# The gated linear unit of two S5 layers: seven products of halves in place of two column passes

## The chip, the cores and the metric

The kernel runs on one core of a Trainium2 chip. TensorE (PE) multiplies, VectorE (DVE) and ScalarE (ACT) work element by element, GpSimd (POOL) does a little arithmetic and issues transfers, and SyncE (SP) only issues transfers. The metric is the time of one launch in device microseconds; a shown time is the median of several runs, and the profile is one separate execution.

## The reference

The kernel is a trunk of four layers for one sequence of 512 tokens and 1024 features, in float32. Layers 0 and 3 mix with S5, layer 1 with gated linear attention, layer 2 with differential attention; behind every mixer comes a feed-forward network (FFN). The change concerns the end of the S5 mixer:

```python
    y = y + d_skip.astype(f32) * h.astype(f32)
    z = jax.nn.gelu(y).astype(h.dtype)
    a, b = jnp.split(z @ w_glu, 2, axis=-1)
    return a * jax.nn.sigmoid(b)
...
    x = x + mix.astype(x.dtype)
    h = rmsnorm(x, norm_ffn[layer])
    x = x + swiglu_ffn(h, ffn_w_gate_up[layer], ffn_w_down[layer]).astype(x.dtype)
```

z is 512 x 1024 and w_glu is 1024 x 2048: columns 0 to 1023 give the values a, columns 1024 to 2047 the gates b.

## The kernel before

Every float32 matmul is done in parts. A weight tile is loaded by SP (`staged`, L357), ACT writes its rounded high part (`high`, L368), and DVE writes the rest as the low part (`low`, L376). `mm3` (L396 to L398) then multiplies high by high, high by low and low by high into one PSUM bank. The transposed z (`zT`) is kept in both parts. One weight tile of two blocks of 128 rows by 512 columns (512 KB, an element count of 128x1024) serves 2 x 4 x 3 = 24 matmuls of 128x512: two blocks of K, four blocks of 128 tokens (t), three part products. A pass over 512 columns is four such tiles, 96 matmuls.

The GLU has four passes. The first (gate columns 1024 to 1535) runs inside the S5 code before; `s5_glu` receives its four banks and takes their tanh. Then come, in `s5_glu`: value columns 0 to 511, gate columns 1536 to 2047, and value columns 512 to 1023. Sigmoid is written with tanh. Behind a value pass DVE multiplies (L1884) and adds the result to the residual x (L1886). For each t the updated x goes on into the FFN's left side (`Sides`): ACT squares it for the norm (L114), PE transposes it in four pieces (`put`, L123, into one of two `tp` banks), ACT scales the pieces from PSUM into `halves` (`keep`, L211), and once two t are there, their high and low parts are made (L206, L207). The FFN's own matmuls (L565) are already seven products of halves.

The program order of every engine in `s5_glu` is set by a scheduler from dependences up to the last pass's tail; from there it is written out (`hand_all` in `gemm_b`'s tail), the first two FFN weight tiles are staged and split ahead of that tail (`ahead(2)`), and the last four blocks of K are done t by t, so that x of t = 0 is ready while PE still multiplies for the other t. FFN weights that are sums of two tiles come as a plain load by SP and a second, accumulating transfer issued by POOL (L598, L601).

## Time and profile before

| | |
|---|---|
| median of 3 runs | 2273.99 us (2273.94 to 2277.14) |
| the profiled execution | 2275.25 us, of which its span 2273.2 us |
| granted TensorE clock | 0.991 |
| busy share of the span | PE 97%, DVE 69%, ACT 49%, POOL 12% |
| GLU of layer 0 in `s5_glu` | about 157 to 226 us of the span |
| GLU of layer 3 in `s5_glu` | about 1855 to 1924 us |

A row of the timeline gives the start, the duration, the engine, the source line, the operation, the tile written and the tiles read, and in brackets the engine's idle time before it and what ended that. A row of the groups gives busy time and the mean of one, then the idle time before. Tile names have no numbers there. PE matmuls are pipelined: a row's duration is longer than the step from one to the next. In a windows row stand the busy time and the number of instructions of PE, PE's weight loads, DVE, ACT and POOL, the granted clock, the busy share of the transfer engines and the rate.

### The profile page before, as it was taken

To read this page: it belongs to the slowest core of one execution; us is meant where nothing else is said; L and a number is where in the kernel's file an instruction comes from. 1 tells how busy PE (TensorE), PEld (TensorE's weight loads), DVE (VectorE), ACT (ScalarE), POOL (GpSimd) and SP (SyncE) were. 2 spreads that over 40 slices of the span, in tenths; PEclk is the share of its full clock that TensorE was granted. 3 is DMA by queue.
4 is the path that set the end of the run, shared out by engine and by line. 5 is a ranking of instruction groups with operands and counts; after the bars stand their busy time and mean duration, and the time that the engine had idled before them with its cause. 6 is when DMAs were issued, how large, how long until landed. Compare 5 with 4: busy or idle time off the path is not lost.

```text
span 2273.2 us, 37225 instructions
## 1 busy us (share of the span) xinstructions
PE 2201.9 (97%) x14847; PEld 1954.2 (86%) x14847; DVE 1561.0 (69%) x2420; ACT 1120.6 (49%) x1870; POOL 282.6 (12%) x392
## 2 busy tenths in 40 slices
PE   5999999999999999999999999999999899999997
PEld 3878979889777799998988887999998888989896
DVE  8963978776625479777745775977766954957574
ACT  6534645454453456555435675644444234635342
POOL 1000141521000011101002231111000001101000
PEclk8999999999999999999999999999999999999999
DMA  4257476663422557766237365976531646767521
GB/s 88 51 153 187 114 194 160 171 187 84 123 74 74 143 144 181 193 161 164 93 126 158 93 151 139 244 208 148 169 92 45 159 131 158 195 158 181 152 76 65
DMA packets 295463, 317.83 MB, mean 140 GB/s; under 512 B 72221, under 2 KB 235353, under 8 KB 294906
## 3 DMA queue, kind: packets, MB, share of 16 engines
q1 hardware_dynamic: 233050, 234.23, 34.1%
q0 software_dynamic: 62240, 81.22, 19.2%
q8 instruction: 117, 1.92, 0.4%
q14 instruction: 56, 0.46, 0.1%
HBM read 283.54 MB, written 16.65 MB: 132 GB/s over the span
## 4 chain that ended last, share of the span: by engine, by line
PE 82%; DVE 8%; ACT 4%; issue 3%; DMA 2%; SPq 1%; POOL 0%; ACTq 0%; DVEq 0%; POOLq 0%
PE a L565 18%; PE acc L396 14%; PE acc L398 13%; PE acc L397 13%; PE c L565 8%; PE d L565 4%; PE y L1481 2%; DVE whl L376 2%; ACT whl L368 1%; PE s L2309 1%; PE V L1445 1%; PE op L2343 1%; PE tp L123 1%; DVE halves L229 1%; ACT halves L211 1%
## 5 line engine op out<-in xcount | busy, mean ns | idle before, releaser
L376 DVE TENSOR_TENSOR whl<-wst,whl 128x1024 fp32r<-128x1024 f32 x272 | 331.4, 1223 | 258.1 <-ACT whl L368 257.1
L368 ACT CAST whl<-wst 128x1024 fp32r<-128x1024 f32 x272 | 283.9, 1050 | 306.8 <-PE acc L398 227.8
L565 PE MATMUL a<-side,whl 128*128 128x256 f32 x3168 | 382.7, 277 | 4.1 <-DVE whl L376 3.6
L565 PEld LDWEIGHTS a<-side,whl 128*128 128x128 f32 x3168 | 369.4, 188 | 6.9 <-DVE whl L376 5.5
L396 PE MATMUL acc<-whl,act 128*128 128x512 f32 x704 | 278.3, 396 | 1.7 <-DVE x L548 1.7
L397 PE MATMUL acc<-whl,act 128*128 128x512 f32 x704 | 274.7, 390 | 0.0
L398 PE MATMUL acc<-whl,act 128*128 128x512 f32 x704 | 274.6, 390 | 0.0
L565 PE MATMUL c<-side,whl 128*128 128x256 f32 x2112 | 254.3, 277 | 1.2 <-DVE whl L376 1.2
L565 PEld LDWEIGHTS c<-side,whl 128*128 128x128 f32 x2112 | 246.7, 188 | 2.0 <-DVE whl L376 2.0
L376 DVE TENSOR_TENSOR whl<-slot,whl 128x1024 fp32r<-128x1024 f32 x107 | 130.5, 1222 | 70.5 <-ACT whl L368 70.5
L396 PEld LDWEIGHTS acc<-whl,act 128*128 128x128 f32 x704 | 132.1, 188 | 32.1 <-issue 2.6
L398 PEld LDWEIGHTS acc<-whl,act 128*128 128x128 f32 x704 | 132.2, 188 | 27.9
L397 PEld LDWEIGHTS acc<-whl,act 128*128 128x128 f32 x704 | 132.2, 188 | 25.7
L368 ACT CAST whl<-slot 128x1024 fp32r<-128x1024 f32 x107 | 112.2, 1053 | 82.8 <-PE acc L398 35.1
L396 PE MATMUL acc<-whl,hT 128*128 128x512 f32 x352 | 142.3, 404 | 0.0
L398 PE MATMUL acc<-whl,hT 128*128 128x512 f32 x352 | 138.2, 393 | 0.0
L397 PE MATMUL acc<-whl,hT 128*128 128x512 f32 x352 | 138.0, 392 | 0.0
L565 PE MATMUL a<-sides,whl 128*128 128x256 f32 x1056 | 134.4, 283 | 0.0
L565 PEld LDWEIGHTS a<-sides,whl 128*128 128x128 f32 x1056 | 129.7, 191 | 1.1
L565 PE MATMUL d<-sides,whl 128*128 128x256 f32 x1056 | 126.6, 276 | 1.0 <-ACT whl L368 1.0
L565 PEld LDWEIGHTS d<-sides,whl 128*128 128x128 f32 x1056 | 122.9, 188 | 1.2 <-ACT whl L368 1.2
L704 ACT CAST act<-r 128x512 fp32r<-128x512 f32 (+1 forms) x110 | 66.4, 646 | 115.4 <-DVE r L683 108.0
(458 smaller groups left out, 3872.0 us busy)
## 6 DMA issues: line engine op xcount, KB each, us to landing
wst<-in_ffn_w_gate_up_dram SPq DMA_DIRECT2D x88, 512.0 KB, 5.0
wst<-in_ffn_w_down_dram SPq DMA_DIRECT2D x88, 512.0 KB, 4.2
slot<-in_ffn_w_gate_up_dram SPq DMA_DIRECT2D x71, 512.0 KB, 5.5
wst<-in_ffn_w_gate_up_dram POOLq DMA_DIRECT2D x44, 512.0 KB, 6.1
halves<-in_ffn_w_gate_up_dram SPq DMA_DIRECT2D x43, 512.0 KB, 5.4
wst<-in_s_w_glu_dram SPq DMA_DIRECT2D x32, 512.0 KB, 4.5
wst<-in_gla_w_in_dram SPq DMA_DIRECT2D x24, 512.0 KB, 3.7
wst<-in_diff_w_qkv_dram SPq DMA_DIRECT2D x24, 512.0 KB, 4.4
```

Of the source, the lines that this page charges most:

```text
L123: tr.nc.tensor.transpose(p[:, j], h[:, j * P : (j + 1) * P], tr.ident[:])
L211: self.tr.nc.scalar.mul(self.F[t // 2, d][:, j, (t % 2) * P : (t % 2 + 1) * P], p[:, j], self.gcol[:, 4 * d + j : 4 * d + j + 1])
L229: v.tensor_tensor(s, s, y, op=op)
L368: self.last["high"] = self.nc.scalar.copy(hl[:, 0], w[:])
L376: self.last["low"] = self.nc.vector.tensor_tensor(hl[:, 1], w[:], hl[:, 0].bitcast(F32), op=ALU.subtract)
L396: mm(out, lh, rh, start=first, stop=False)
L397: mm(out, lh, rl, start=False, stop=False)
L398: self.last["mm"] = mm(out, ll, rh, start=False, stop=last)
L565: mm(o, hl[:, x, k, c], side[y][:, k], start=first and not (j or k or n), stop=k == 3 and n == 2, skip_group_check=True,)
L704: self.last["act high"] = nc.scalar.copy(dst[:, 0, j], src[:, j])
L1445: mm(V[kk][z][:, bs(b)], inm[:, z, bs(b)], U[:, bs(b)], start=True, stop=True)
L1481: mm(yb[:, b], q[:, j, b], om[:, j // 2, bs(b)], start=False, stop=j == 3)
```

## The change

The first column pass in `s5_glu` (values 0 to 511, now L458 to L460) stays: 96 matmuls. The two passes over value columns 512 to 1023 and gate columns 1536 to 2047, 192 matmuls, become seven products of halves. Tokens are halved (t = 0, 1 and t = 2, 3), K is halved, and the two column blocks are the halves of the weight. Each product has 2 t x 4 blocks of K x 3 parts = 24 matmuls of 128x512 (L1986), 168 in all.

What feeds them is new. The class `WideSides` makes the left sides. POOL adds high and low of a quarter of zT back together (`joined`, L269), DVE forms the sums "1" to "4" (L287, L288, L293, L304), and ACT and DVE split each again (`parts`, L273, L274). The weights' sums are formed by transfers: SP loads a piece into `wsum` or `third` (L1974), POOL's accumulating transfer adds another (L1979), eight of these per layer. `wsum` holds in turn three sums (product "1", then "2", then "4"), each by accumulating on the last. `third` (product "3") is a new tile in the storage of `wide1`, the left side of product "1". Weight splits (L430 high, L438 low) are 18 per layer in place of 12. PSUM results are copied to SBUF by ACT (L1997) and combined by DVE (L2055, L2062, L2069); the gate (L1992, L1994) and the tanh (L1996) follow. `gated` now writes multiply and add for each t in turn. The two FFN heads (`ahead(2)`) are written before the combination r2. The order on all five engines is written out for the whole of `s5_glu`.

The order of the products on PE is: first pass, 11 ("11" is the weight piece and the left quarter), 1, 2, 12 with 21, 3, 4 with 22, 22 with the sum "4"; the transposes of x for the last three t stand inside or behind the last product.

Here is the diff, cut to its core:

```diff
+class WideSides:
...
+    def __init__(self, tr, pool, hT, spare):
+        self.tr, self.hT = tr, hT
+        self.m = pool.tile([P, 4, 256], F32, name="summand")
+        self.y = {n: pool.tile([P, 2, 4, 256], F32R, tag="wide" + n, name="wide" + n) for n in ("1", "4", "3", "2")}
+        self.s = spare[:].rearrange("p (k n) -> p k n", n=256)
...
+    def joined(self, out, name, ks=slice(0, 4)):
+        hi, lo = (self.quarter(name, z)[:, ks].bitcast(F32) for z in range(2))
+        self.tr.nc.gpsimd.tensor_tensor(out, hi, lo, op=ALU.add)
+    def parts(self, name, src, ks=slice(0, 4)):
+        hi, lo = (self.side(name, z)[:, ks] for z in range(2))
+        self.tr.nc.scalar.copy(hi, src)
+        self.tr.nc.vector.tensor_tensor(lo, src, hi.bitcast(F32), op=ALU.subtract)
+    def whole(self, then):
+        self.u = [(slice(k, k + 2), self.tr.np_.tile([P, 2, 256], F32, tag="hh", name="wideu")) for k in (0, 2)]
+        self.joined(self.m[:], "22")
+        self.joined(self.s, "21")
+        then()
+        for ks, u in self.u:
+            self.joined(u[:], "11", ks)
+    def first(self):
+        v = self.tr.nc.vector
+        for ks, u in self.u:
+            v.tensor_tensor(u[:], u[:], self.s[:, ks], op=ALU.subtract)
+        v.tensor_tensor(self.s, self.s, self.m[:], op=ALU.subtract)
+        self.parts("1", self.s)
+    def second(self):
+        for ks, u in self.u:
+            self.tr.nc.vector.scalar_tensor_tensor(
+                self.s[:, ks], u[:], -1.0, self.m[:, ks], op0=ALU.mult, op1=ALU.subtract
+            )
+        self.joined(self.m[:], "12")
+        self.parts("2", self.s)
+    def third(self):
+        for ks, u in self.u:
+            self.parts("3", u[:], ks)
+    def fourth(self):
+        self.tr.nc.vector.tensor_tensor(self.s, self.s, self.m[:], op=ALU.add)
+        self.parts("4", self.s)
...
         v = nc.vector
         wg = self.i["s5_w_glu"][L]
         nxt = Sides(self, 3 * L, self.i["ffn_w_gate_up"][3 * L])
+        mm = nc.tensor.matmul
+        cols = (512, D + 512)
+        self.hand_all()
         with self.tc.tile_pool(name=f"s5g_{L}", bufs=1) as p:
-            for d in range(2):
...
-                stat = lambda k, part, t: zT[:, part, k, t * P : (t + 1) * P]
-                if d == 0:
-                    for t in range(NT):
-                        evac_b(t, accs[t])
-                else:
-                    self.gemm_b(stat, wg, KT, D + d * 512, evac_b)
-                ahead = (lambda: (nxt.ahead(2), nxt.total("3"))) if d else None
-                with nullcontext() if d else self.tc.issue_after(self.last_turned.ins):
-                    self.gemm_b(stat, wg, KT, d * 512, evac_a, tail=4 if d else 0, ahead=ahead)
+            self.edge(p, 64)
...
+            sums = WideSides(self, p, zT, nxt.g)
+            wide = p.tile([P, 4, 512], F32, name="wsum")
+            half = lambda y, b: y[:, 2 * b : 2 * b + 2]
+            piece = lambda q, c, b: self.wb_src(wg, 4 * q + 2 * b, cols[c])
+            W, H = {}, {}
+            for b in range(2):
+                W[f"1{b}"] = W[f"2{b}"] = W[f"4{b}"] = half(wide, b)
+            def stage(*names):
+                for n in names:
+                    b = int(n[-1])
+                    src = self.wb_src(wg, 2 * b, 0) if n[0] == "w" else piece(int(n[0]) - 1, int(n[1]) - 1, b)
+                    W[n] = self.staged(src, 2, 512)
...
+            def both(y, name, one, two):
+                for b in range(2):
+                    nc.sync.dma_start(half(y, b), piece(*one, b))
+                return lambda: plus(y, two)
+            def plus(y, two):
+                for b in range(2):
+                    nc.gpsimd.dma_start(half(y, b), piece(*two, b), accum_op=ALU.add)
+            def product(side, name, bank, first, t, ks=range(4)):
+                st = sums.stat(side)
+                for k in ks:
+                    hl = H[name + str(k // 2)]
+                    for n, (x, y) in enumerate(((0, 0), (0, 1), (1, 0))):
+                        mm(
+                            bank[t][:], st(k, x, t), hl[:, y, k % 2], start=first and not (k or n),
+                            stop=k == 3 and n == 2, skip_group_check=True,
+                        )
+            def gated(t, d, th, value):
+                v.scalar_tensor_tensor(th, th, 1.0, value, op0=ALU.add, op1=ALU.mult)
+                xs = self.x[:, t, d * 512 : (d + 1) * 512]
+                v.scalar_tensor_tensor(xs, th, 0.5, xs, op0=ALU.mult, op1=ALU.add)
+            tanh = lambda y, src=None: nc.scalar.activation(y, y if src is None else src, AF.Tanh, scale=0.5)
+            copy = lambda y, bank: [nc.scalar.copy(y[z][:], bank[z][:]) for z in range(2)]
+            stage("w0", "w1", "w2")
+            summed = both(wide, "1", (0, 1), (0, 0))
+            sums.whole(summed)
+            split("w0", "w1")
+            for t in range(NT):
+                tanh(gate[t][:], accs[t][:])
+            stage("w3", "110", "111", "210")
+            split("w2", "w3", "110")
+            sums.first()
+            split("111")
+            sums.second()
+            split("10", "11")
+            plus(wide, (1, 1))
+            sums.third()
+            stage("211")
+            banks = [self.acc() for t in range(NT)]
+            for k in range(KT):
+                for t in range(NT):
+                    ts = slice(t * P, (t + 1) * P)
+                    hl = H[f"w{k // 2}"]
+                    self.mm3(
+                        banks[t][:], zT[:, 0, k, ts], zT[:, 1, k, ts], hl[:, 0, k % 2], hl[:, 1, k % 2],
+                        k == 0, k == KT - 1,
+                    )
+                    if k == KT - 1:
+                        gated(t, 0, gate[t][:], banks[t][:])
+                        nxt.take(t, 0)
+            r1, r5 = ([line("gate", 4) for z in range(2)] for y in range(2))
+            a, c = ([self.acc() for z in range(2)] for y in range(2))
+            d = [self.sbank("d") for z in range(2)]
+            product("11", "11", a, True, 0)
+            self.flush()
+            product("11", "11", a, True, 1)
+            split("210")
+            copy(r1, a)
+            split("20")
+            for t in range(2):
+                product("1", "1", c, True, t)
+            third = p.tile([P, 4, 512], F32, tag="wide1", name="third")
+            W.update({f"3{b}": half(third, b) for b in range(2)})
+            summed = both(third, "3", (0, 1), (1, 1))
+            stage("220", "221")
+            split("21")
+            sums.fourth()
+            copy(r5, c)
+            for t in range(2):
+                product("2", "2", a, False, t)
+            summed()
+            plus(wide, (1, 0))
+            split("211", "30")
+            copy(r2, a)
+            for t in range(2):
+                product("12", "21", d, True, t)
+            split("31", "220")
+            for z in range(2):
+                v.tensor_tensor(r1[z][:], r1[z][:], d[z][:], op=ALU.add)
+            split("221")
+            for t in range(2):
+                product("3", "3", a, False, t)
+            split("40")
+            nxt.total("3")
+            for z in range(2):
+                v.tensor_tensor(r5[z][:], r5[z][:], a[z][:], op=ALU.subtract)
+                tanh(r5[z][:])
+            split("41")
+            for t in range(2):
+                product("4", "22", c, False, t)
+            nxt.ahead(2)
+            for z in range(2):
+                v.tensor_tensor(r2[z][:], c[z][:], r2[z][:], op=ALU.subtract)
+                tanh(r2[z][:])
+                gated(z, 1, r2[z][:], r1[z][:])
+                if z == 0:
+                    nxt.take(0, 1)
+            product("22", "4", a, False, 0, range(2))
+            nxt.take(1, 1)
+            product("22", "4", a, False, 0, range(2, 4))
+            gated(2, 1, r5[0][:], a[0][:])
+            product("22", "4", a, False, 1, range(2))
+            nxt.take(2, 1)
+            product("22", "4", a, False, 1, range(2, 4))
+            gated(3, 1, r5[1][:], a[1][:])
+            nxt.take(3, 1)
         return nxt
```

**SP, the loads in the second half of the GLU of layer 0.** Rows with their waits: DVE, PE and Pool are engines, DMAHW and DMASW are transfers by SP and by POOL. `wst` is a staged weight, `slot0` an FFN weight. Before:

```order
L357 DMA wst_1824<-in_s5_w_glu_dram 128x2x512 [waits DMAHW6_49,DVE_49]
L357 DMA wst_1865<-in_s5_w_glu_dram 128x2x512 [waits DMAHW7_49,DVE_49]
L357 DMA wst_1894<-in_s5_w_glu_dram 128x2x512 [waits DMAHW0_49,DVE_49]
L357 DMA wst_1923<-in_s5_w_glu_dram 128x2x512 [waits DMAHW1_49,DVE_49]
L357 DMA wst_1928<-in_s5_w_glu_dram 128x2x512 [waits DMAHW2_49,DVE_49]
L357 DMA wst_1935<-in_ffn_w_gate_up_dram 128x4x256 [waits DMAHW3_49,DVE_49]
L357 DMA wst_1937<-in_ffn_w_gate_up_dram 128x4x256 [waits DMAHW4_49,DVE_49]
```

and now:

```order
L419 DMA wst_1598<-in_s5_w_glu_dram 128x2x512 [waits DMAHW7_49,DVE_49]
L419 DMA wst_1634<-in_s5_w_glu_dram 128x2x512 [waits DMAHW0_49,DVE_49]
L1974 DMA third_1856<-in_s5_w_glu_dram 128x2x512 [waits DVE_49,PE_49]
L1974 DMA third_1856<-in_s5_w_glu_dram 128x2x512 [waits DMAHW5_49]
L419 DMA wst_1859<-in_s5_w_glu_dram 128x2x512 [waits DMAHW6_49,DMAHW1_49,DVE_49]
L419 DMA wst_1861<-in_s5_w_glu_dram 128x2x512 [waits DMAHW2_49,DVE_49]
L419 DMA wst_2004<-in_ffn_w_gate_up_dram 128x4x256 [waits DMAHW3_49,DVE_49]
```

The loads of `third` wait for PE (the storage of `wide1`), and the weight loads for product "22" (1859, 1861) and the FFN's loads are queued behind them. The next place is ACT at the same point; 1902 and 1931 are the high parts of `third`, 1966 that of the last `wsum`, `r2` the copies of the accumulator that product "3" then adds to, gate_1774 and gate_1775 hold r5:

```order
L430 CAST whl_1899<-wst_1634 128x1024
L430 CAST whl_1902<-third_1856 128x1024
L1997 COPY r2_1558<-acc_1776 128x512
L1997 COPY r2_1559<-acc_1777 128x512
L430 CAST whl_1931<-third_1856 128x1024
L430 CAST whl_1934<-wst_1859 128x1024
L430 CAST whl_1939<-wst_1861 128x1024
L430 CAST whl_1966<-wsum_1565 128x1024
```

Before, ACT had only high parts of plain loads at this point. The copies of `r2` must come before product "3" adds on in the same banks, and they are queued behind the first high part of `third`.

**DVE, the last work before x of t = 0 of the second column half.** Before (1930 is the last weight of the GLU, 1939 and 1942 are the FFN's heads):

```order
L376 TENSOR_TENSOR whl_1930<-wst_1928,whl_1930 128x1024
L376 TENSOR_TENSOR whl_1939<-wst_1935,whl_1939 128x1024
L376 TENSOR_TENSOR whl_1942<-wst_1937,whl_1942 128x1024
L225 TENSOR_TENSOR s3_1945<-halves_1545 128x512
L225 TENSOR_TENSOR s3_1947<-halves_1545 128x512
L1884 SCALAR_TENSOR_TENSOR gate_1844<-gate_1844,acc_1861 128x512
L1886 SCALAR_TENSOR_TENSOR x_1541<-gate_1844,x_1541 128x512
```

and now (2008 and 2011 are the FFN's heads, 1966 and 1977 the low parts of the last `wsum`, `acc_1776` the bank of product "3", `acc_1778` that of product "4"):

```order
L438 TENSOR_TENSOR whl_1939<-wst_1861,whl_1939 128x1024
L438 TENSOR_TENSOR whl_1966<-wsum_1565,whl_1966 128x1024
L225 TENSOR_TENSOR s3_1969<-halves_1545 128x512
L225 TENSOR_TENSOR s3_1971<-halves_1545 128x512
L2062 TENSOR_TENSOR gate_1774<-gate_1774,acc_1776 128x512
L2062 TENSOR_TENSOR gate_1775<-gate_1775,acc_1777 128x512
L438 TENSOR_TENSOR whl_1977<-wsum_1565,whl_1977 128x1024
L438 TENSOR_TENSOR whl_2008<-wst_2004,whl_2008 128x1024
L438 TENSOR_TENSOR whl_2011<-wst_2006,whl_2011 128x1024
L2069 TENSOR_TENSOR r2_1558<-acc_1778,r2_1558 128x512
L1992 SCALAR_TENSOR_TENSOR r2_1558<-r2_1558,gate_1772 128x512
L1994 SCALAR_TENSOR_TENSOR x_1541<-r2_1558,x_1541 128x512
```

The FFN's heads stand between the last split and the first multiply in both, but two subtractions (L2062), a further split and the r2 subtraction (L2069) have come between.

**PE, behind the first column pass.** Before, `tp` for t = 0 and 1 follows the first matmul of the next pass:

```order
L398 MATMUL acc_1562<-whl_1652,zT_91 128x512
L396 MATMUL acc_1715<-whl_1721,zT_91 128x512
L123 MATMUL tp_1688<-ident_78,x_1541 128x128 x4
L123 MATMUL tp_1704<-ident_78,x_1541 128x128 x4
L397 MATMUL acc_1715<-whl_1721,zT_91 128x512
L398 MATMUL acc_1715<-whl_1721,zT_91 128x512
```

and now:

```order
L459 MATMUL acc_1638<-whl_1603,zT_91 128x512
L460 MATMUL acc_1638<-whl_1603,zT_91 128x512
L123 MATMUL tp_1745<-ident_78,x_1541 128x128 x4
L458 MATMUL acc_1639<-whl_1603,zT_91 128x512
L459 MATMUL acc_1639<-whl_1603,zT_91 128x512
L460 MATMUL acc_1639<-whl_1603,zT_91 128x512
L123 MATMUL tp_1761<-ident_78,x_1541 128x128 x4
L1986 MATMUL acc_1776<-whl_1606,zT_91 128x512 x6
L1986 MATMUL acc_1776<-whl_1614,zT_91 128x512 x6
L123 MATMUL tp_1794<-ident_78,x_1541 128x128 x4
L123 MATMUL tp_1803<-ident_78,x_1541 128x128 x4
```

The first transposes stand ahead of the last three matmuls of the pass, the second behind them, and the third and fourth 12 matmuls later, inside the first of the seven products.

30 lines of the change are left out of this document (21 added, 9 removed).

## The prediction

> **What bounds the kernel now.** I read the head of the page first, then the chain of waits, then windows around the GLU, then the timeline and groups there. The page:
>
> ```profile
> span 2273.2 us, 37225 instructions
> PE 2201.9 (97%) x14847; PEld 1954.2 (86%) x14847; DVE 1561.0 (69%) x2420; ACT 1120.6 (49%) x1870; POOL 282.6 (12%) x392
> PE 82%; DVE 8%; ACT 4%; issue 3%; DMA 2%; SPq 1%; POOL 0%; ACTq 0%; DVEq 0%; POOLq 0%
> ```
>
> PE bounds the whole. The windows show what that means at the change: the first pass of layer 0, its two last passes, the FFN behind it, and the last passes of layer 3.
>
> ```profile
> 157.00:179.00 22.00, 22.00 (x99) 18.22 (x98) 9.60 (x10) 7.37 (x9) 0.00 (x0) 1.00 0.60 186
> 179.00:227.00 48.00, 47.98 (x229) 39.71 (x228) 18.61 (x23) 22.17 (x53) 5.10 (x4) 1.00 0.77 200
> 227.00:262.00 35.00, 34.81 (x305) 34.62 (x304) 31.48 (x36) 22.19 (x33) 6.28 (x8) 1.00 0.41 95
> 1877.00:1925.00 48.00, 47.98 (x228) 39.69 (x227) 18.62 (x23) 21.85 (x52) 5.18 (x4) 1.00 0.71 180
> ```
>
> PE never stands still in either GLU and the clock is full: every matmul saved there is time, and every wait added is time. DVE works 28 of 70 us there. Behind it the FFN has 0.2 us of PE's idle time in 35, so it can give nothing back and hide nothing late.
>
> **What is removed.** The step of a 128x512 matmul comes from two rows of the timeline 12 matmuls apart:
>
> ```profile
> 215.23 0.39 PE L396 MATMUL acc<-whl,zT 128*128 128x512 f32 x1
> ...
> 217.95 0.39 PE L396 MATMUL acc<-whl,zT 128*128 128x512 f32 x1
> ```
>
> 2.72 / 12 = 0.227 us. Per layer 192 matmuls become 168: 24 x 0.227 = 5.4 us, 10.9 us for both. That is all the change can gain.
>
> **What is added, and whether it is hidden.** Prices of the element-wise work:
>
> ```profile
> L376 DVE TENSOR_TENSOR whl<-wst,whl 128x1024 fp32r<-128x1024 f32 x16 | 19.5, 1223 | 29.2 <-ACT whl L368 29.2
> L368 ACT CAST whl<-wst 128x1024 fp32r<-128x1024 f32 x16 | 16.7, 1051 | 26.5 <-PE acc L398 22.6 <-DMA wst<-in_s_w_glu_dram 3.9
> L114 ACT ACTIVATE sq<-x 128x512 f32<-128x512 f32 x8 | 5.0, 631 | 8.6 <-DVE x L1886 8.6
> L114 ACT ACTIVATION_READ_ACCUMULATOR sq<-x 128x1 f32 x8 | 1.5, 192 | 0.0
> L1881 ACT ACTIVATE gate<-acc 128x512 f32<-128x512 f32 x8 | 4.6, 600 | 2.6 <-PE acc L398 2.3
> ...
> 186.02 1.23 DVE L207 TENSOR_TENSOR sides<-halves,sides 128x1024 fp32r<-128x1024 f32 x1 [2.61 <-ACT sides L206]
> 187.16 1.22 DVE L376 TENSOR_TENSOR whl<-wst,whl 128x1024 fp32r<-128x1024 f32 x1
> 210.86 1.29 DVE L225 TENSOR_TENSOR s<-halves 128x512 f32<-128x512 f32 x2
> 217.52 0.69 DVE L1886 SCALAR_TENSOR_TENSOR x<-gate,x 128x512 f32<-128x512 f32 x1
> 219.32 0.60 PE L123 MATMUL tp<-ident,x 128*128 128x128 f32 x4
> 219.96 1.14 ACT L211 ACTIVATE halves<-tp,gffn 128x128 f32<-128x128 f32 x4 [0.99 <-PE tp L123]
> ```
>
> Back to back, a 1024-wide DVE operation steps by 1.14 (186.02 to 187.16), a 512-wide one by 0.62 to 0.65. Per layer DVE gets six weight splits, four side splits, the sums and six combinations, 18 to 20 us, ACT about 14. Both have that much room on average; where PE waits is a matter of place, and I went through the four places in program order.
>
> *Behind the first pass.* DVE reaches the first gate just as its bank is done. It goes multiply, add, multiply, add, each pair 1.38 us; PE has six matmuls (1.36) until the first transposes and three with four transposes (about 1.14) until the second: it waits 0.4 and 0.2. The third and fourth follow after 12 matmuls, not 24, with only two `tp` banks; the fourth needs the second emptied, which ACT does behind four squares of 0.82 and two times 1.14: 1.3 us late. Together **1.9 us**.
>
> *Product "3".* Its weight can be loaded only when product "1" has freed the storage, 48 matmuls = 10.9 us ahead of use. Transfers of 512 KB, by SP, then accumulating ones by POOL, for one layer, then the latter one by one (issued at 202.3, 204.9 and, nearly alone, 233.7):
>
> ```profile
> wst<-in_s_w_glu_dram SPq DMA_DIRECT2D x9, 512.0 KB, 4.3
> ...
> lent<-in_ffn_w_gate_up_dram POOLq DMA_DIRECT2D x1, 512.0 KB, 8.6
> ...
> lent<-in_ffn_w_gate_up_dram POOLq DMA_DIRECT2D x1, 512.0 KB, 10.4
> ...
> slot<-in_ffn_w_gate_up_dram POOLq DMA_DIRECT2D x1, 512.0 KB, 6.0
> ...
> wst<-in_s_w_glu_dram SPq DMA_DIRECT2D x1, 512.0 KB, 3.8
> ```
>
> A load nearly alone lands in 3.8 (the last row, issued at 183.4). The first accumulating one takes between 6.0 and 10.4; I take 7.2, nearer the lower end, since before it had up to seven SP loads beside it and here four. Then ACT's high part, and behind it in ACT's queue the copy of r2 that frees the bank: 3.8 + 7.2 + 0.2 + 1.0 + 0.6 = 12.8, so PE waits 1.9; its second matmul waits 0.6 for the low part. The second accumulating transfer lands about 4 us behind the first (the two rows above: 204.9 + 10.4 less 202.3 + 8.6 is 4.4), PE has 1.4 us of matmuls until it needs it: 1.8 for the high part and 1.0 for the low. Together **5.3 us**; 1 us if both transfers cost nothing, 11 at 10.4.
>
> *The last gate's x of t = 0.* This is DVE's own queue, as its order in the section on the change has it. From the start of the low part of the second half of `third`, up to x: seven 1024-wide splits (two of them FFN heads) 7 x 1.14 = 8.0; seven 512-wide sums 4.4; multiply and add 1.4; tanh of r2 with its handover 0.7; and 1.6 of waiting for ACT, whose high part of the last sum is queued behind the two tanh of r5 (0.6 each). Sum 16.1. PE starts 1.3 behind that point and has 5 + 12 + 24 + 6 = 47 matmuls, 10.7: it stands at the transposes at 12.0 and waits **4.2 us**. Before, the FFN heads were split while PE worked through the pass; here they lie on the path and are 2.3 of the 4.2. Faster transfers do not shorten it, since both sides start from the same split; they only start it sooner.
>
> *The start of the FFN.* x of the last t goes through the same two `tp` banks: about **0.7 us**, an estimate from the 1.14 of L211 and the square ahead of it.
>
> Sum of a layer: 1.9 + 5.3 + 4.2 + 0.7 = 12.1 lost, 5.4 gained: +6.7. Layer 3 has the same instructions and the same windows: +13.4 in all. The profiled execution's 2275.25 becomes 2288.6; it lies 1.26 above the median of the runs shown, so the same sum there gives 2287.4. I say **2288**.
>
> *POOL's additions.* They are in none of these terms as long as DVE has its first sums in time. The trace has no wide addition on POOL. Nearest rows:
>
> ```profile
> L1930 POOL MEMSET wa<- 128x512 f32 x1 | 0.5, 528 | 0.0
> masks.py:199 POOL TENSOR_SCALAR_AFFINE_SELECT ident<-ident 128x128 f32<-128x128 f32 x1 | 0.3, 284 | 0.1
> masks.py:197 POOL MEMSET ident<- 128x128 f32 x1 | 0.2, 205 | 0.3 <-POOLq L2527 0.3
> L1037 POOL TENSOR_SCALAR nident<-ident 128x128 fp32r<-128x128 f32 x1 | 0.6, 596 | 0.1
> ```
>
> A 1024-wide one costs at least DVE's 1.22 and at most 8 x 0.596 = 4.8. I take 2.4: the MEMSETs give 0.1 fixed and 0.84 ns an element; the select with one input 1.4 ns an element; a second input I put at another 0.84 (estimate). DVE needs the additions of 22, 21 and both halves of 11 in a row, three wide ones, from 155 on: at 2.4 plus two transfer issues they are there at 164.6, and from then DVE is without slack until the gate at 177.2. Each 0.1 us more per addition delays that gate by 0.3 us. [...]
>
> **Rivals.**
>
> *Hidden: faster.* Both halves of `third` are split 4.2 us or more before PE comes to them. Then the second term is gone, and the third too, since DVE is ahead by as much (behind product "4" of t = 0 it has 2.8 us of work and PE 18 matmuls, 4.1). What is left, 2.6, is less than the 5.4 saved: 2.8 gained a layer, 2275.3 - 5.6 = 2270; with every wait hidden 2264. For it: the average room on DVE and ACT. Against it: of the 10.9 us between the two products the load takes 3.8, the split 2.3, which leaves 0.6 for the accumulating transfer where the quickest row has 6.0.
>
> *Near.* Accumulating transfers at 6.0 and the second 2 us behind: the second term 2; DVE gets between none and half of that head start: the third 2 to 4. Net +1.2 to +3.3 a layer: 2278 to 2282.
>
> *DVE held up by POOL.* While POOL adds, DVE has three weight splits in the same stretch, with operands in the same memory. If the two exclude one another, these 3.4 us come later, and the first gate with them; PE waits 3.4 more a layer: 2288 + 7 = 2295. [...] No row of before has the two side by side. The additions at 3.6 instead of 2.4 do the same (+3.6 a layer), at 4.8 twice that: 2303.
>
> *Queue.* Transfers by POOL at 10.4 each: the second term at 11 rather than 5.3, +11 in all: 2299.
>
> **How the numbers follow.** The forecast (the sum, 2282 to 2293) 0.52; held up by POOL 0.22; near 0.13; hidden 0.08; queue 0.05. About 0.2%, 4.5 us, is what a measurement of this kernel can tell from no change; half of near falls inside. Faster 0.08, same 0.07, slower 0.85. The range leaves out hidden and the lower part of near, and POOL's dearest case: 2277 to 2302.
>
> **What would show it.** Right: PE's idle time of about 12 us in each GLU, with DVE's x (L1994) in front of L123, and ACT's `whl` from `third` in front of L1986; 24 fewer matmuls a GLU at 0.227 still; the FFN's window unchanged. The loads of `third` issued the moment product "1" ends. POOL's L269 at 2.4 for 1024 elements, and DVE's splits beside it at 1.22 still; if they are 2 us and more, or start late with L269 in front, the POOL rival holds. Wrong: PE without gaps at product "3" (accumulating transfers faster than any row), or DVE ahead of the transposes at t = 0, which would need its splits to step by less than 1.14; or time lost in the FFN, which I put at nothing.

## The result

The changed kernel takes 2303.49 us (median; 2301.55 to 2304.83) against 2275.22 us of the kernel before on the same chip (2273.94 to 2277.14): a ratio of 1.0123, 95% interval [1.0111, 1.0135], 28 us slower. The direction was forecast, the size was not: +13.4 was the sum, 2302 the upper end of the range.

The profiled execution of the changed kernel, 2301.55 us, its page:

```profile
span 2299.7 us, 37280 instructions
PE 2203.3 (96%) x14799; PEld 1950.5 (85%) x14799; DVE 1612.1 (70%) x2466; ACT 1146.3 (50%) x1904; POOL 320.3 (14%) x418
PE 79%; DVE 10%; ACT 4%; issue 3%; DMA 3%; SPq 1%; POOL 0%; ACTq 0%; DVEq 0%; POOLq 0%
```

PE does 48 matmuls fewer and is busy for 1.4 us *more*: saved matmuls should have taken 10.9 us off. That is the first sign that the matmuls that are left became slower. The windows of the changed kernel, GLU of layer 0, the FFN behind it, and the GLU of layer 3 (columns as before; the granted clock is the third from the end):

```profile
155.00:180.00 25.00, 22.97 (x102) 18.69 (x100) 19.23 (x15) 11.19 (x14) 12.96 (x9) 1.00 0.54 142
180.00:240.00 60.00, 49.84 (x212) 40.00 (x213) 33.28 (x40) 31.44 (x65) 10.70 (x9) 0.89 0.82 199
240.00:275.00 35.00, 34.08 (x297) 33.70 (x296) 32.28 (x37) 22.17 (x35) 6.53 (x9) 1.00 0.71 156
1885.00:1945.00 60.00, 47.48 (x196) 37.40 (x195) 35.74 (x40) 31.07 (x58) 10.18 (x8) 0.89 0.56 135
```

PE stands still where it never did, and the clock is 0.89 in both GLUs where every row of before had 1.00. The waits of PE in the GLU of layer 0, in sum, times and longest:

```profile
PE acc L1986 <- ACT r L1997: 4.1, 1, 4.1
PE tp L123 <- issue: 4.1, 1, 4.1
PE tp L123 <- DVE x L1994: 3.9, 1, 3.9
PE acc L458 <- ACT zT L1556: 0.7, 1, 0.7
PE tp L123 <- ACT whl L430: 0.3, 1, 0.3
```

Three waits of about 4 us (in layer 3 they are 4.1, 4.6 and 3.6). Two are those of the prediction: product "3" (L1986, for the copies of r2 behind the high part of `third`) and the transposes in the last product (for DVE's x). The one that the view puts down to "issue" is the transposes behind the first pass, forecast at 0.4; DVE's x comes at 181.94 (below) and PE goes on at 182.04.

To compare kernels without what varies from run to run elsewhere, I measured in each trace the time from the first matmul behind the S5 code's last transposes of z (12 matmuls ahead of the first pass) to the start of the FFN's 481st product matmul, "the stage". Before: 131.0 in layer 0 and 131.2 in layer 3. Changed: 145.3 and 144.8, so +14.3 and +13.6, 27.9 in all; from the end of the stage of layer 0 to the start of that of layer 3 it is 1567.4 before and 1566.4 after, and behind that of layer 3 289.4 and 289.6. The whole loss lies in the two stages.

**Where DVE was late.** DVE's timeline in the first pass, and POOL's:

```profile
158.50 7.85 DVE L438 TENSOR_TENSOR whl<-wst,whl 128x1024 fp32r<-128x1024 f32 x3 [4.21 <-ACT whl L430]
...
174.62 2.52 DVE L274 TENSOR_TENSOR wide<-spare,wide 128x1024 fp32r<-128x1024 f32 x1 [1.12 <-ACT wide L273]
...
180.54 0.68 DVE L1992 SCALAR_TENSOR_TENSOR gate<-gate,acc 128x512 f32<-128x512 f32 x1
181.25 0.69 DVE L1994 SCALAR_TENSOR_TENSOR x<-gate,x 128x512 f32<-128x512 f32 x1
```

```profile
156.79 2.40 POOL L269 TENSOR_TENSOR spare<-zT 128x1024 f32<-128x1024 f32 x1
159.14 2.42 POOL L1979 DMA_DIRECT2D wsum<-in_s_w_glu_dram  x2
160.70 3.42 POOL L269 TENSOR_TENSOR wideu<-zT 128x512 f32<-128x512 f32 x2
173.65 2.41 POOL L269 TENSOR_TENSOR summand<-zT 128x1024 f32<-128x1024 f32 x1 [9.52 <-DVE spare L293]
```

POOL's addition takes 2.40, as I had put it. But three splits of DVE, which should take 3.5 us in a row (1.22 and two steps of 1.14), take 7.85, and another takes 2.52, each ending 1.1 us behind the end of a POOL addition (160.70 + 3.42 = 164.12, and DVE's second split, 5.02 long, ends at 165.22; 173.65 + 2.41 = 176.06, and DVE's 174.62 + 2.52 = 177.14). The first gate comes at 180.54 instead of the 177.2 of the prediction, in a stage that began 0.6 us earlier than the one of before.

**Where PE was slow.** PE's timeline in the last product, and the windows of 5 us there:

```profile
230.53 1.11 PE L123 MATMUL tp<-ident,x 128*128 128x128 f32 x4 [3.91 <-DVE x L1994]
231.29 5.16 PE L1986 MATMUL acc<-whl,zT 128*128 128x512 f32 x12
```

```profile
225.00:230.00 5.00, 1.61 (x8) 0.99 (x6) 4.27 (x6) 1.76 (x3) 2.38 (x2) 0.91 0.94 223
230.00:235.00 5.00, 4.47 (x13) 3.70 (x14) 3.18 (x6) 3.04 (x9) 0.00 (x0) 0.50 1.18 237
```

Behind the wait of 3.9 us the clock is 0.50; twelve matmuls take 5.16 instead of 12 x 0.227 + 0.16 = 2.9 us. The step from one to the next is 0.43 for nine of them. The same stands behind the other two waits, for three to six matmuls. Finer windows of the same view have 0.50 from 181.4 to 184.8, from 212.1 to 215.5 and from 229.1 to 236.0, and 1.00 right ahead of and behind each: the half clock came in stretches of 3.4, 3.4 and 6.8 us, and began while PE still waited or just as it went on. Where PE goes on (182.04, 211.95 and 230.53), 2.7, 3.5 and 5.4 us of them are left; three matmuls are slow behind the first of these waits, nine behind the last. In layer 0 the steps that are longer than they should be add up to some 4.5 us.

### The profile page after: what moved, and what is told of

The parts are those of the page before. It is cut to its first block, busy times and chain, and to the rows that moved or that the text cites. A ratio compares the mean times of both kernels' runs of the same rounds, so it can differ in the third digit from the quotient of the medians.

```text
span 2299.7 us, 37280 instructions
## 1 busy us (share of the span) xinstructions
PE 2203.3 (96%) x14799; PEld 1950.5 (85%) x14799; DVE 1612.1 (70%) x2466; ACT 1146.3 (50%) x1904; POOL 320.3 (14%) x418
## 4 chain that ended last, share of the span: by engine, by line
PE 79%; DVE 10%; ACT 4%; issue 3%; DMA 3%; SPq 1%; POOL 0%; ACTq 0%; DVEq 0%; POOLq 0%
PE a L627 17%; PE acc L458 12%; PE acc L460 12%; PE acc L459 12%; PE c L627 8%; PE d L627 4%; DVE whl L438 2%; PE acc L1986 2%; PE y L1543 2%; DMA third<-in_s_w_glu_dram 1%; ACT whl L430 1%; PE s L2494 1%; PE op L2528 1%; PE tp L123 1%; PE V L1507 1%
## 5 line engine op out<-in xcount | busy, mean ns | idle before, releaser
L438 DVE TENSOR_TENSOR whl<-wst,whl 128x1024 fp32r<-128x1024 f32 x268 | 334.1, 1253 | 216.1 <-ACT whl L430 215.5
L430 ACT CAST whl<-wst 128x1024 fp32r<-128x1024 f32 x268 | 279.2, 1050 | 260.9 <-PE acc L460 176.4
L458 PE MATMUL acc<-whl,act 128*128 128x512 f32 x704 | 278.3, 396 | 1.6 <-DVE x L610 1.6
L460 PE MATMUL acc<-whl,act 128*128 128x512 f32 x704 | 274.7, 390 | 0.0
L438 DVE TENSOR_TENSOR whl<-slot,whl 128x1024 fp32r<-128x1024 f32 x107 | 130.5, 1223 | 68.2 <-ACT whl L430 68.1
L458 PEld LDWEIGHTS acc<-whl,act 128*128 128x128 f32 x704 | 132.1, 188 | 32.0 <-issue 2.6
L460 PEld LDWEIGHTS acc<-whl,act 128*128 128x128 f32 x704 | 132.1, 188 | 28.0
L459 PEld LDWEIGHTS acc<-whl,act 128*128 128x128 f32 x704 | 132.2, 188 | 25.6
L430 ACT CAST whl<-slot 128x1024 fp32r<-128x1024 f32 x107 | 112.2, 1053 | 82.0 <-PE acc L460 34.2
L458 PE MATMUL acc<-whl,hT 128*128 128x512 f32 x352 | 142.5, 405 | 0.0
L460 PE MATMUL acc<-whl,hT 128*128 128x512 f32 x352 | 138.0, 392 | 0.0
L627 PEld LDWEIGHTS a<-sides,whl 128*128 128x128 f32 x1056 | 129.8, 191 | 0.9
```

What stands on the lines that cost most here:

```text
L430: self.last["high"] = self.nc.scalar.copy(hl[:, 0], w[:])
L438: self.last["low"] = self.nc.vector.tensor_tensor(hl[:, 1], w[:], hl[:, 0].bitcast(F32), op=ALU.subtract)
L458: mm(out, lh, rh, start=first, stop=False)
L459: mm(out, lh, rl, start=False, stop=False)
L460: self.last["mm"] = mm(out, ll, rh, start=False, stop=last)
L627: mm(o, hl[:, x, k, c], side[y][:, k], start=first and not (j or k or n), stop=k == 3 and n == 2, skip_group_check=True,)
```

## The experiments

Theories after the two traces: **A**, DVE's splits and POOL's additions shut one another out, which makes the first wait; **B**, behind each long wait PE runs at half its clock; **C**, the transfers of `third` make the wait of product "3", and DVE's queue that in the last product, as predicted. The rivals: DVE is late by the length of its own queue; the long steps come from contention; the waits hang together, so that one taken away comes back as another.

| kernel | median us | stage of layer 0 | stage of layer 3 |
|---|---|---|---|
| before | 2274.3 to 2275.7 | 131.0 | 131.2 |
| the change | 2303.5 | 145.3 | 144.8 |
| additions on DVE | 2294.5 | 141.2 | 140.4 |
| three waits filled | 2302.3 | 142.3 | 143.7 |
| last wait filled | 2299.6 | 143.2 | 142.3 |
| `third` in storage of its own | 2288.1 | 136.6 | 136.3 |
| FFN heads later | 2298.2 | 141.6 | 142.7 |
| additions on DVE + own storage | 2278.2 | 132.6 | 132.2 |
| + FFN heads later | 2272.3 | 129.6 | 129.8 |
| + split 41 earlier | 2271.8 | 129.4 | 130.4 |
| + other order in memory | 2280.1 | 131.1 | 134.3 |
| + that, and transposes later | 2278.5 | 130.3 | 134.9 |
| + transposes later, old order | 2271.7 | 128.4 | 131.3 |
| + transposes later, third order | 2268.4 | 127.7 | 127.7 |

### The additions on DVE

```diff
-        self.tr.nc.gpsimd.tensor_tensor(out, hi, lo, op=ALU.add)
+        self.tr.nc.vector.tensor_tensor(out, hi, lo, op=ALU.add)
...
-            sums.whole(summed)
             split("w0", "w1")
+            sums.whole(summed)
```

> Theory A: the four additions of quarters on POOL and the two-input operations of DVE shut one another out; DVE splits of 1.78, 5.02 and 2.52 us stand exactly beside the additions. Here the additions are done by DVE itself, behind the splits of the first two weights, where DVE idles 4.2 us, and the last one in a 1.1 us wait for ACT. A expects: every split 1.22, the first gate (L1992) at about 177.3 instead of 180.5, the wait ahead of the first transposes 0.4 to 0.8 instead of 4.1, no half-speed matmuls behind it (0.75 us): about 4 us a layer, 8 in all, 2295. Rival (DVE is late through the length of its own queue, POOL has nothing to do with it): 4.9 us more on DVE's queue bring the first gate later, 2305 to 2312.

2294.46 us, ratio to before 1.0085 [1.0070, 1.0100]. DVE's timeline at the same place:

```profile
155.58 1.23 DVE L269 TENSOR_TENSOR summand<-zT 128x1024 f32<-128x1024 f32 x1
156.73 1.22 DVE L269 TENSOR_TENSOR spare<-zT 128x1024 f32<-128x1024 f32 x1
157.86 1.29 DVE L269 TENSOR_TENSOR wideu<-zT 128x512 f32<-128x512 f32 x2
159.80 3.50 DVE L438 TENSOR_TENSOR whl<-wst,whl 128x1024 fp32r<-128x1024 f32 x3 [0.66 <-ACT whl L430]
...
178.04 0.68 DVE L1992 SCALAR_TENSOR_TENSOR gate<-gate,acc 128x512 f32<-128x512 f32 x1
```

The three splits take 3.50 instead of 7.85. Counted from the start of the stage (154.9 here, 153.6 in the change), the first gate comes at 23.2 instead of 26.9. The wait ahead of the first transposes is 0.3 instead of 4.1, and no slow step stands behind it. Only then the wait between the third and fourth transposes shows that the prediction had (1.3 there; 0.9 here). A holds, at 9.0 us; the rival, by which 4.9 us more work on DVE would make it later, falls. It is not POOL's issuing of transfers either: two issues (157.43 to 159.85) stand beside DVE's additions here, and these take 1.2 to 1.3 as anywhere. All this is about the splits; that every operation of DVE with two inputs is held up so, as the expectation has it, was not shown.

The trace of before had rows that point at A, which I overlooked; they stand in layer 1, and there it is POOL that waits:

```profile
592.39 0.23 POOL L1920 TENSOR_SCALAR_AFFINE_SELECT mask<-mask 64x64 f32<-64x64 f32 x1
592.69 0.79 POOL L1920 TENSOR_SCALAR_AFFINE_SELECT mask<-mask 64x64 f32<-64x64 f32 x1
592.70 0.68 DVE L107 TENSOR_TENSOR hh<-x,gain 128x512 f32<-128x512 f32 x1
```

The same select takes 0.23, and then 0.79 beside a DVE multiply; it ends 0.1 behind the multiply's end. In the trace of the change this multiply begins 0.04 behind the second select; there the select takes 0.23 and the multiply 0.73. So either engine can be the one that waits. Which of them it is does not follow from these starts alone: DVE's split of 5.02 us starts at 160.20, ahead of the two additions (from 160.70) that it sits through, though spans on POOL are rough.

### The waits filled with useless matmuls

```diff
+            def junk(n):
+                y = self.tp("junk")
+                for i in range(n):
+                    mm(y[:].rearrange("p a b -> p (a b)"), zT[:, 0, 0, :P], zT[:, 0, 0], start=True, stop=True)
...
+                        if t == 2:
+                            junk(16)
                         nxt.take(t, 0)
...
+            junk(16)
             for t in range(2):
                 product("3", "3", a, False, t)
...
             product("22", "4", a, False, 0, range(2))
+            junk(15)
             nxt.take(1, 1)
```

> Theory B: behind each wait of about 4 us PE runs at half its clock for a while (steps of 0.43 us instead of 0.227, some 4.5 us a layer in sum). Here useless matmuls into a free bank fill most of the three waits of each layer: 16 ahead of the first transposes, 16 ahead of product 3, 15 ahead of the transposes in the last product (94 matmuls of 128x512 more in all, results not read, nothing left out). B expects: granted clock 1.00 throughout, steps of 0.227 behind the waits, the waits end when they did; what the half speed cost behind the first and the last wait comes back, behind product 3 it is taken up by the next wait: 3 us a layer, 5 to 7 in all, 2297. Rival (the long steps come from contention or late operands, not from the clock): no gain, or up to 2 us lost.

2302.33 us (2300.05 to 2305.58), which the change's own spread of 3 us does not tell from it. The mechanism shows in the windows all the same:

```profile
180.00:185.00 5.00, 4.52 (x22) 3.25 (x21) 4.93 (x8) 0.96 (x3) 2.40 (x2) 1.00 0.62 96
210.00:215.00 5.00, 4.65 (x20) 3.15 (x18) 1.22 (x1) 2.42 (x4) 0.00 (x0) 1.00 1.12 208
230.00:235.00 5.00, 4.41 (x22) 3.42 (x21) 3.89 (x6) 3.00 (x9) 0.18 (x1) 1.00 1.16 232
```

The clock is 1.00 at all three places, with nothing but PE's idleness changed; contention as the cause falls, since nothing of the transfers or of the other engines' work was taken away. The stages are 4.1 us shorter in sum, of 5 to 7 expected. Behind product "3" nothing comes back: with the steps short again, PE waits 0.5 and 0.8 for the two parts of the second half of `third` (0.9 and 0.8 in layer 3). To price it where nothing behind can take it up, only the last wait was filled.

> Only the last of the three waits of each layer is filled, with 15 useless matmuls ahead of the transposes in the last product; the changed kernel otherwise. Behind that wait nothing hides PE's half speed. Theory B: the half-speed steps behind it vanish, the first transposes to the first FFN product take 5.4 us in both layers as with all three filled (changed kernel: 7.9 and 6.7); 3.8 us in all, 2299.7. Rival (the waits behind take it up): 0.

2299.63 us (2296.68 to 2303.62), 3.9 less than the change by the medians and as expected, but the runs of the two kernels overlap. The traces are clearer: the stages are 4.6 us shorter in sum, with 30 matmuls more. PE's timeline:

```profile
228.65 3.57 PE L1999 MATMUL junk<-zT 128*128 128x512 f32 x15
232.05 0.60 PE L123 MATMUL tp<-ident,x 128*128 128x128 f32 x4
232.41 3.02 PE L1986 MATMUL acc<-whl,zT 128*128 128x512 f32 x12
```

The twelve matmuls behind the wait take 3.02, not 5.16. B holds, at some 4 us in all: that is what the half clock costs at the end. What it costs behind the first two waits (some 2 us a layer) is mostly lost in the next wait anyway: with all three filled the stages gained no more, 4.1. In the stages of all these kernels half rate stood behind waits from 2.1 us (layer 3 of the kernel with the transposes later in the old order, below) to 4.6 us (layer 3 of the change); behind waits of 0.7 and 1.1 us (the kernel with the heads later, below) the clock was 1.00.

### `third` in storage of its own

```diff
-            r2 = [line("r2", 2) for z in range(2)]
             sums = WideSides(self, p, zT, nxt.g)
+            r2 = [sums.m[:].rearrange("p a b -> p (a b)")[:, 512 * z : 512 * z + 512] for z in range(2)]
...
             sums.third()
+            third = p.tile([P, 4, 512], F32, name="third")
+            W.update({f"3{b}": half(third, b) for b in range(2)})
+            both(third, "3", (0, 1), (1, 1))()
             stage("211")
...
-            third = p.tile([P, 4, 512], F32, tag="wide1", name="third")
-            W.update({f"3{b}": half(third, b) for b in range(2)})
-            summed = both(third, "3", (0, 1), (1, 1))
             stage("220", "221")
...
-            summed()
             plus(wide, (1, 0))
```

> Theory C: product 3 waits for the transfers of its weight, which start only when product 1 has freed the storage. Here that weight has storage of its own (r2 lies in the summand's, free by then) and is loaded and accumulated during the first pass. C expects: the 4.3 us ahead of product 3, its 1.0 us of smaller waits and 1.3 us of half speed vanish; DVE's queue gets ahead, so that the wait in the last product shrinks from 4.1 to between 0 and 2, with its half speed: 8 to 11 us a layer, 2282 to 2287. Rival (the DVE queue bounds product 3 and the tail, the transfers only fall together with it): 0 to 4 us a layer, 2296 to 2303.

2288.06 us, ratio to before 1.0051 [1.0034, 1.0068]: 15.4 less than the change, its stages 17.2 less, and 1 us above the range that C gave. PE's waits now, and its timeline in the last product:

```profile
PE tp L123 <- issue: 4.0, 1, 4.0
PE tp L123 <- DVE x L1994: 2.4, 1, 2.4
PE acc L458 <- ACT zT L1556: 0.7, 1, 0.7
PE tp L123 <- ACT whl L430: 0.3, 1, 0.3
```

```profile
226.45 0.66 PE L123 MATMUL tp<-ident,x 128*128 128x128 f32 x4 [2.44 <-DVE x L1994]
226.86 4.58 PE L1986 MATMUL acc<-whl,zT 128*128 128x512 f32 x12
```

The wait of product "3" is gone, and the last one shrank from 3.9 to 2.4: DVE had been held up by the transfers as well (in the change it sat idle for 9.6 us ahead of the first split of `third`, here not at all), yet 2.4, where C gave 0 to 2, is its own queue (in the kernel with the additions and the heads moved as well, below, no wait over 1 us is left there). C holds, a little short. The 2.4 still has half speed behind it (4.58 for the twelve).

### The FFN heads behind the first gates

```diff
-            nxt.ahead(2)
             for z in range(2):
                 v.tensor_tensor(r2[z][:], c[z][:], r2[z][:], op=ALU.subtract)
...
                     nxt.take(0, 1)
+            nxt.ahead(2)
```

> The prediction had 2.3 of 4.2 us of the last wait come from splitting the two FFN heads ahead of the combination r2. Here they are written behind the first two gates. Prediction's mechanism: the wait falls from 4.1 to 1.8; with theory B the half speed behind it (2.5 us) goes too, since 1.8 is as short as waits that show none: 4 to 4.8 us a layer, 2294; without B 2.3 a layer, 2299. Up to 1 us a layer may be lost again where the FFN starts. Rival (the wait ends by a PE or ACT event, not by DVE's queue): no change.

2298.15 us (2295.29 to 2301.61), 5.3 less than the change; stages 5.8 less. The waits of layer 0:

```profile
PE tp L123 <- issue: 4.1, 1, 4.1
PE acc L1986 <- ACT r L1997: 3.8, 1, 3.8
PE tp L123 <- DVE x L1994: 1.8, 2, 1.1
```

The last wait falls from 3.9 to 0.7 and leaves no slow steps (the clock is 1.00 from 225 to 240); but the heads now stand ahead of the third gate, and the third transposes wait 1.1 for it. By the stages 3.7 us were gained in layer 0 and 2.1 in layer 3, less than the 4 to 4.8 a layer with B, because a part is given back in a new wait, which I had put at the FFN's start instead. The runs spread over 6 us, so the median alone does not tell 2298 from the 2299 without B.

### The edits together

Each next kernel has the last one's edits and one more: additions on DVE with the storage, then the heads, then the split "41" ahead of r5 (`split("40", "41")`).

> The additions on DVE and the storage of its own for the weight of product 3, together. If the two losses are separate (theories A and C), the gains add: by the medians 2303.5 - 9.0 - 15.4 = 2279; what is left is the wait in the last product (2.6 us a layer with the storage alone, then 1.3 of half speed) and smaller ones, just above the 10.9 us of saved matmuls. Rival (one wait takes up what the other gives): 2285 to 2288.

2278.19 us, ratio 1.0016 [1.0006, 1.0025]. 2303.5 - 9.0 - 15.4 = 2279.1: the gains add, so the first wait and that of product "3" are separate losses and not one that moves.

> Both of these and the FFN heads behind the first two gates. With product 3 on time the last wait of 2.6 us is all DVE's queue, and the heads are 2.3 of it: no wait over 1 us left ahead of the transposes, no half speed; 3 to 4 us a layer, some lost again at the start of the FFN: 2272 to 2275, level with the kernel before or up to 0.15% under it. Rival (the heads' splits then stop the transposes or the FFN for as long): 2278 to 2280.

2272.30 us, ratio 0.9991 [0.9981, 1.0000]; as expected.

> As the last, and the second half of the last weight sum is split ahead of the subtraction r5 and its two tanh, so that DVE no longer waits 1.6 us for ACT there. If the path to x of t = 0 still decides: 0.5 to 1.5 us a layer less, 2270 to 2273. If it no longer does: the same as the last.

2271.80 us, ratio 0.9987 [0.9977, 0.9996]. It is 0.5 us less than the last and not told from it; the split that I moved waits for PE now (3.0 us of idle time at ACT's high part), apparently for a buffer of `whl`, and no longer stands behind the two tanh.

The FFN's first product starts 2.4 to 3.0 us earlier than in the kernel before, but 480 matmuls later 0.9 to 1.6 are left: the FFN's first summed weights (`lent`) lie where the GLU's left sides lay, and SP loads them only when PE has read these. SP's timeline of this kernel:

```profile
204.51 0.50 SPq L660 DMA_DIRECT2D slot<-in_ffn_w_gate_up_dram  x1
216.45 0.37 SPq L660 DMA_DIRECT2D lent<-in_ffn_w_gate_up_dram  x1
216.99 0.39 SPq L660 DMA_DIRECT2D slot<-in_ffn_w_gate_up_dram  x1
```

Two tries put the tiles in another order: `wsum` first, then the left sides as 1, 2, 3, 4; the second also has the transposes of `self.flush()` behind the whole product "11".

> As the kernel with four edits, and the tiles of the GLU stand in another order in memory, so that the FFN's first summed weights fall on storage that is free after products 1 and 2 and not on the left sides of the last product; their loads need not wait for PE. In the four edits' kernel the FFN starts 2.4 to 3.0 us earlier than in the kernel before and is only 0.9 to 1.6 us ahead 480 matmuls on. If the late loads take the rest: 1 to 1.5 us a layer back, 2269. If not: 2271.8 as before.

> As the last, and the third and fourth transposes of the first column half 12 matmuls later, behind the whole first product. Their wait of 1.05 us (for ACT to empty the second bank) should vanish: 1 us a layer less again, 2267; if another wait behind takes it up: as the last.

2280.08 and 2278.47 us, ratios 1.0022 [1.0014, 1.0031] and 1.0016 [1.0007, 1.0024]: a miss, 8 and 7 us worse than 2271.8. `lent` was free early, but now the plain load ahead of it in SP's queue (`slot`) fell on the left side of product 4 and held all behind it. It is issued 11.6 us later than above, and `lent` no earlier:

```profile
199.21 4.88 SPq L419 DMA_DIRECT2D wst<-in_ffn_w_gate_up_dram  x2
216.08 0.37 SPq L660 DMA_DIRECT2D slot<-in_ffn_w_gate_up_dram  x1
216.50 0.50 SPq L660 DMA_DIRECT2D lent<-in_ffn_w_gate_up_dram  x1
```

From the FFN's first product matmul to its 481st the first of the two takes 1.7 us (layer 0) and 4.4 us (layer 3) longer than the kernel with four edits. Late FFN weights do cost microseconds, which the last pair uses:

> The kernel with four edits (2271.8) and the third and fourth transposes behind the whole first product; storage as it was. With the other storage this moved the start of the FFN 0.55 us forward in each layer: 2270.5, and the wait of 1.05 us between two transposes is gone. If the FFN's late weights take all of it: 2271.8.

> The same, with the four left sides of the GLU in another order in memory: the FFN's first plain load now falls on wide1, its first summed weights on wide2 and wide3 (free after product 3, some 5 us ahead of wide4 as it was). Unlike in the last attempt, the load at the head of SP's queue waits for nothing late. If the late weights take 1.4 us a layer in the FFN: 2268. If another wait in SP's queue stands in for it (slot1 on the last weight sum): 2270, as the one above.

```diff
-        self.y = {n: pool.tile([P, 2, 4, 256], F32R, tag="wide" + n, name="wide" + n) for n in ("1", "4", "3", "2")}
+        self.y = {n: pool.tile([P, 2, 4, 256], F32R, tag="wide" + n, name="wide" + n) for n in ("2", "3", "4", "1")}
```

The transposes alone, with the old order in memory: 2271.65 us, ratio 0.9985 [0.9977, 0.9994], nothing gained by the median. In its trace the stage of layer 0 is 1.0 us shorter. That of layer 3 is 1.0 longer: a load of a GLU weight landed there after 9.5 us (7.0 in the next kernel), and PE waits 2.1 us ahead of the first transposes, with the clock at 0.50 behind. With the left sides in the order 2, 3, 4, 1: 2268.39 us, ratio 0.9978 [0.9968, 0.9987], the fastest, 5.9 under the kernel before beside it. SP loads `lent` 5 us earlier, counted from the start of the stage, and the windows (last passes and products of layer 0, FFN, layer 3) are nearly full again:

```profile
210.82 0.37 SPq L660 DMA_DIRECT2D lent<-in_ffn_w_gate_up_dram  x1
```

```profile
179.00:227.00 48.00, 46.68 (x230) 38.30 (x229) 34.44 (x41) 33.70 (x69) 8.56 (x7) 1.00 0.84 190
227.00:262.00 35.00, 34.51 (x302) 34.32 (x301) 31.51 (x36) 22.18 (x32) 7.66 (x9) 1.00 0.87 209
1877.00:1925.00 48.00, 47.02 (x247) 39.70 (x247) 33.56 (x38) 35.18 (x74) 7.05 (x7) 1.00 0.82 194
```

Its stages are 127.7 each, 6.7 less than before in sum, of the 10.9 that the seven products save. They are 4.3 shorter than those of the kernel with the old order, but only 0.9 of this lies in the FFN, where late weights act; the rest is that wait in layer 3. So the order is worth 3.3 us by the medians of 11 runs each, and the traces show the FFN's weights as the reason for 0.9 of it. Whether the late landing comes from the order of the tiles or from that one execution is open.

## Why the prediction was right and wrong

*What is removed.* 24 matmuls a layer at 0.227: right. The stages of the last kernel are 6.7 shorter, of the 10.9.

*Behind the first pass, 1.9 us.* It measured 4.1 in each layer, all ahead of the first transposes. The sum was about right for a DVE that arrives on time: with the additions off POOL the same place has 0.4, 0.2 and 1.0, counted from start to start. What failed is the sentence that POOL's additions are in none of the terms as long as DVE has its first sums in time. The price of an addition was right (2.4 taken, 2.40 measured); that it stops DVE beside it was only a rival, at 0.22, with 3.4 us a layer. The gate came 3.7 later than with the additions on DVE (26.9 against 23.2), and the additions cost 9.0 in all by the median, with the half speed behind that wait. The order had the two engines side by side; I let it weigh as a doubt that no row of before had them so. That was a misreading: the select of 0.79 beside L107 is such a row.

*Product "3", 5.3 us.* 4.1 in layer 0 and 4.6 in layer 3, and 0.6 to 0.8 more at two later matmuls (beyond their half speed): right within 0.6. It stands ahead of the first half instead of in four pieces: the plain load took 4.8, not 3.8, the first accumulating transfer 8.5, not 7.2, and the second landed 2.9 behind it, not 4. That the sum still fits is in part luck, since these misses cancel.

*The last gate's x, 4.2 us.* 3.9, and the list of DVE's operations is that of the trace: from the low part of the second half of `third` (214.40) to the end of x (230.47) it takes the 16.1 of the sum, and PE stands at the transposes 12.0 behind that point. "Faster transfers do not shorten it" was wrong: with the storage of its own it fell to 2.4, since DVE could then work ahead of PE.

*The FFN's start, 0.7 us.* 0.45 in layer 0.

*Slips in the sums.* 16.1 less 12.0 is 4.1, not 4.2, and the terms of "near" add up to +1.2 to +3.2. The 11 us of "queue" are more than its listed terms give with 10.4 in place of 7.2, which is 8.5. None of these changes the account.

*What was not in the sum at all.* The clock. The windows of before showed 1.00 in every row, and PE hardly waited in them; I carried that over to a kernel in which I myself had forecast waits of several microseconds. Some 4 us of the 28 are the half speed behind the last wait, by the filled one, and more may be in the 9.0 and the 15.4, which no run separates.

Put together by medians: 2303.5 - 9.0 (POOL and DVE) - 3.9 (half speed at the end) = 2290.6, against 2288 forecast; by the stages 27.9 - 8.5 - 4.6 = 14.8 lost, against 13.4. This is a sum and not a run: no kernel has these two edits alone. The forecast was short by a rival weighed too low and by a mechanism left out. The range, 2277 to 2302, took in the rival but not the two together.

## What to carry to other kernels

Moving work to an idle engine is no gain where the engine that it is to relieve stands still meanwhile: here POOL's four additions a layer held DVE up by 5.6 us (7.85 and 2.52 instead of 3.50 and 1.23), more than the 5.0 that it needs to do them itself in its own gaps. In these stages PE's waits of 2.1 to 4.6 us cost twice, once for the wait and once for the slow matmuls behind it, at a clock of 0.50. Waits of 0.7 and 1.1 us (the kernel with the heads later) left no slow matmul, so a long wait that is broken up may cost less, which no run tried; but in the attention layer of the changed kernel three waits of 1.4, 0.9 and 0.8 us within 6 us (1394 to 1399) were followed by a clock of 0.50 (1400 to 1403). Here a tile that took over another's storage tied its load to the old tile's last reader (`third` was issued at 197.00, as product "1" ended, and PE waited 4.1 us for what came behind it), and in SP's queue everything behind it too (a `slot` issued 11.6 us later held `lent`): look at who reads last before choosing a tag or an order of allocation.

## What the runs showed of the hardware that was not expected

- Twelve 128x512 matmuls took 5.16 us behind an idle time of 3.9 us and 3.02 behind the same time filled with useless matmuls; the granted clock was 0.50 and 1.00.
- The clock of 0.50 came in stretches of 3.4 us and, once in each layer of the change, of 6.8 (229.1 to 236.0 and 1922.1 to 1929.0), and already behind a wait of 2.1 us (layer 3 of the kernel with the transposes later in the old order).
- A DVE split of 1.22 us takes up to 5.0 us beside POOL's additions, longer than any one of these (2.40): it sat through two in a row. In another place POOL waits: its select of 0.23 us takes 0.79 beside a DVE multiply of 0.68.
- The placement of four equal tiles in memory alone was worth 3.3 us by the medians (2271.7 against 2268.4), of which the traces explain 0.9; another order of all the GLU's tiles cost 8.
